# Eight single PSUM banks in one ring from the up-projection on, and the order of the final weights' rounding, in a hybrid encoder layer on one Trainium2 core

## The chip, the core and the metric

One NeuronCore of a Trainium2 chip runs the whole program. Its engines work at the same time, each through its own instructions in order: TensorE (PE, matrix multiplication; its weight loads are listed apart as PEld), VectorE (DVE), ScalarE (ACT), GpSimd (POOL) and SyncE (SP, which here only issues transfers). Matrix products land in PSUM, eight banks of 512 float32 values for each of the 128 partitions; DVE and ACT read them from there. Everything else lies in SBUF, and weights come from the device memory by DMA.

The metric is the time of one execution on the device in microseconds. A kernel is given by the median of its runs.

## The reference, cut to what matters

The model computes one layer for 512 prompt frames and 64 sample frames, in float32. After an adaLN modulation and a combined input projection come two recurrent mixers, an output projection and a residual. The change lies behind that, in the feed-forward part and the end:

```python
def conv_ffn(h, st, w_up, ffn_conv_w, ffn_conv_b, w_down):
    gate, val = jnp.split(h @ w_up, 2, axis=-1)
    gate_c, new_st = causal_dwconv(gate, st, ffn_conv_w)
    act = jax.nn.silu(gate_c + ffn_conv_b) * val
    return act @ w_down, new_st
...
        h = rmsnorm(x, norm2[l]) * (1 + sc2) + sh2
        f, s_f = conv_ffn(h, ffn_s[l], w_up[l], ffn_conv_w[l], ffn_conv_b[l], w_down[l])
        x = x + g2 * f
...
    y = rmsnorm(x, final_norm)
```

The width is 2048, the feed-forward width 5632, so `w_up` is 2048 x 11264 and `w_down` 5632 x 2048.

## The kernel before, in words

Channels lie on the partitions (16 tiles of 128 for the width, `KD`; 44 for the feed-forward width, `NFF`), frames along the free axis: two halves of 288 (`HT`), each with 256 prompt and 32 sample frames. float32 accuracy comes from splitting both operands into a rounded high part and a low part: ACT rounds (`wh`, line 1631), DVE subtracts (`wl`, line 1633), and PE adds three products, high-high, high-low and low-high (lines 1728 to 1730 in `up_product`, 648 and 650 in `mm6`).

Behind the mixers and the output projection (whose last eight-tile half, lines 2185 to 2192, ends at about 1266 us) the kernel has three stages:

- **Up-projection** (`up`, 44 units t = 0 to 43). Each unit computes one gate tile and one value tile by a Strassen-like scheme with seven products c = 0 to 6 over half of the depth, so each unit has seven sums of weights to prepare (`up_prep`, two steps ahead), seven products and seven outputs (`up_out`). A product is 8 x 3 matmuls. Its seven products go into three sums x, y and z, one PSUM bank each. The activation is written to device memory (`actd`); `pair_put` reads it back two tiles at a time, makes the combinations that the down-projection needs, and stores them (`cd`).
- **Down-projection** (units t = 44 to 75: four groups g of eight units u), the same scheme with 5 x 3 matmuls a product and 40 of the 44 depth tiles. The order of a unit's steps is 0, then step 6 of the unit before, then 2, 1, 3, 4, 5. `down_out` adds each sum to its place in SBUF on DVE (line 1924), in the first group it copies on ACT (line 1922). During units 1 to 4 of the first group `act_put` (lines 1963 to 1982) splits the last four activation tiles and stores them (`ald`). During the last group `down_end` closes the finished tiles on POOL (lines 1949, 1951, 1960) and ACT (line 1959).
- **Final** (`final`): for each half of the frames and each of the 16 output tiles m, PE adds the product of the last four depth tiles (12 matmuls of 320 or 256 columns), DVE adds it, scaled, to the residual (line 2042), and after every fourth m four transposes for each block of frames turn the result (line 2093), followed by the last RMS norm and the stores. `final_w` prepares the weights: for m below 6 by `wtile`, from 6 on into tiles `hw` of their own (ACT line 2065, DVE line 2067).

PSUM has two pools all this time. `pg` (line 110) has two double tiles of two banks each, handed out by `pgt` (line 663); `pm` (line 2139) has four single banks, handed out by `bank` (line 132). The up-projection takes its three sums from `pm`. In the down-projection even units and the last one take three banks of `pm`; odd units take two double tiles of `pg` and use the banks a0 (x), a1 (y) and b0 (z). The final products take a double tile for each two m, the transposes a bank of `pm`.

The order on each engine is made ahead of time by a planner which follows the program's order and its own estimate of times, lets a later instruction go first where an earlier one cannot start, and sets the semaphore waits. `issue_after(i)` holds an instruction behind instruction i on its engine; `high_priority` moves the block up. `self.round_of` and `self.split_of` are the latest weight rounding and subtraction of `up_split`, `self.load_of` the latest weight load.

Of the kernel before, what the change touches and what calls it, by code (L numbers as in the profile page):

```python
# [9 lines left out]
F32R = mybir.dt.float32r  # L10
I32 = mybir.dt.int32
AF = mybir.ActivationFunctionType
ALU = mybir.AluOpType
PSUM = bass.MemoryType.PSUM
# [9 lines left out]
NFF = 44  # L24
# [20 lines left out]
N_UNITS = NFF + KD // 2 * NCH  # L45
# [59 lines left out]
class Kern:  # L105
    def __init__(self, tc, ctx, i, o):
        self.tc, self.nc, self.ctx, self.i, self.o = tc, tc.nc, ctx, i, o
        self.n = 0
        self.cp = ctx.enter_context(tc.tile_pool(name="cp", bufs=1, side="left"))
        self.pg = ctx.enter_context(tc.tile_pool(name="pg", bufs=2, space=PSUM))  # L110
        self.c, self.scrap = {}, []
        self.now, self.chain, self.free = 0.0, None, dict.fromkeys(OP_US, 0.0)
        self.jv, self.ja = _Timed(self, _Sooner(tc, tc.nc.vector), "V"), _Timed(self, _Sooner(tc, tc.nc.scalar), "A")
        self.tv, self.ta = _Timed(self, tc.nc.vector, "V"), _Timed(self, tc.nc.scalar, "A")
        self.jt = _TimedPE(self, tc.nc.tensor)
        self.pool = _Timed(self, _InTurn(tc, tc.nc.gpsimd), "G")
# [1592 lines left out]
    def up_product(self, t, c):  # L1709

        w = HZ if t < NFF else HT
        if c == 0:
            if t < NFF or t % 2 == 0 or t == N_UNITS - 1:
                banks = [self.bank()[:, :w] for _ in range(3)]
            else:
                a, b = self.pgt(), self.pgt()
                banks = [a[:, 0, :w], a[:, 1, :w], b[:, 0, :w]]
            self.a[t, "banks"] = banks
            self.a.pop((t - 2, "banks"), None)
        T, (wh, wl) = self.nc.tensor, self.a.pop((t, "w", c))  # L1720
        ps = self.a[t, "banks"][(0, 2, 1, 0, 1, 2, 1)[c]][:, :HT if c in (T3, B22) else w]
        n = NPAIR if t < NFF else NJ
        for j in range(n):
            hi, lo, _ = self.combos[c, j] if t < NFF else self.dn[(t - NFF) // NPAIR, c, j]

            if c in (T3, B22):
                hi, lo = hi[:, :HT], lo[:, :HT]
            T.matmul(ps, wh[:, j], hi, start=(c < 3 and j == 0), stop=False, skip_group_check=True)  # L1728
            T.matmul(ps, wh[:, j], lo, start=False, stop=False, skip_group_check=True)  # L1729
            T.matmul(ps, wl[:, j], hi, start=False, stop=(j == n - 1), skip_group_check=True)  # L1730
# [232 lines left out]
    def act_put(self, n):  # L1963

        nc = self.nc
        r, f = [self.v_tile().rearrange("p h t -> p (h t)")[:, :2 * HT] for _ in range(2)]
        src, ald = self.actd[NFF - 4 + n], self.ald[n]
        with self.tc.issue_after(self.load_of):
            for h, b in ((0, 0), (1, HL)):
                nc.sync.dma_start(r[:, b:b + HP], src[:, h, :HP])  # L1970
            nc.sync.dma_start(r[:, HP:HL].rearrange("p (h t) -> p h t", h=2), src[:, :, HP:HT])
        yield
        hi = f.bitcast(F32R)
        with self.tc.issue_after(self.round_of):
            nc.scalar.activation(hi, r, AF.Copy)
        with self.tc.issue_after(self.split_of):
            nc.vector.tensor_tensor(r.bitcast(F32R), r, f, op=ALU.subtract)
        yield
        with self.tc.issue_after(self.load_of):
            nc.sync.dma_start(ald[:, 0], f)  # L1980
            nc.sync.dma_start(ald[:, 1], r)
        yield
# [23 lines left out]
    def final(self, acts, free):  # L2006

        wide = lambda n: [free.pop(0) for _ in range(n)]
        self.w_places, self.row_places = wide(20), wide(2)
        self.final_begin()
        w = []
        places = 2 * wide(12)
        late, behind, o = [], {}, self.o
        xs = [self.slot(p, F32, HT).rearrange("p h t -> p (h t)") for p in wide(2)]
        sampled = lambda m: xs[m // 8][:, m % 8 * 2 * HS:(m % 8 + 1) * 2 * HS]
        for h in range(2):
            cols = [(slice(0, HP), 0)]  # L2020
            toks = [(lambda m, h=h, b=b: self.x1[m][:, h, b:b + P], P, o["y_prompt"][0, h * HP + b:h * HP + b + P]) for b in range(0, HP, P)]
            if h == 0:
                cols.append((slice(HP, HL), 1))
                toks.append((sampled, 2 * HS, o["y_sample"][0]))
            span = (slice(0, HL), slice(HL, 2 * HT))[h]
            blocks = [(x, n, [places.pop(0) for _ in range(4)],
                       self.sp.tile([P, 8], F32, tag="fms", bufs=6, name=self.name("fms")), y) for x, n, y in toks]
            for m in range(KD):
                if m == len(w):
                    w += self.final_w(m, behind)  # L2030
                if m % 2 == 0:
                    ps = self.pgt()
                for k in range(4):
                    self.mm6(ps, w[m][0][:, k], w[m][1][:, k], [a[:, :, span] for a in acts[k]], k == 0, k == 3,
                             ((0, span.stop - span.start),), m % 2)
                for c, q in cols:
                    p = ps[:, m % 2, c]
                    if q == 0:
                        x = y = self.x1[m][:, h, c]
                    else:  # L2040
                        x, y, p = self.x1[m][:, :, HP:HT], self.halves(sampled(m)), self.halves(p)
                    self.nc.vector.scalar_tensor_tensor(y, p, self.mod[:, 5, m, q:q + 1], x,
                                                        op0=ALU.mult, op1=ALU.add)
                behind[m + KD * h] = self.nc.cur_bb.bb.instructions[-1]
                if late and m % 4 == LATE:
                    late.pop(0)()
                if m % 4 == 3:
                    late.append(lambda q=m // 4, blocks=blocks: self.final_part(q, blocks))
        while late:
            late.pop(0)()  # L2050

    def final_w(self, m, behind):

        src = self.w_down(NFF - 4, m)
        if m < 6:
            t = self.wtile(src)
            return [[x[:, :, j * P:(j + 1) * P] for x in t] for j in range(2)]
        raw = self.raw().rearrange("p (k n) -> p k n", k=4)
        w = [[pool.tile([P, 4, P], F32R, tag=tag, name=self.name("hw"))
              for pool, tag in self.w_places[2 * j:2 * j + 2]] for j in (m - 6, m - 5)]  # L2060
        with self.tc.high_priority(offset=AHEAD):
            self.nc.sync.dma_start(raw, src)
            for j, (hi, lo) in enumerate(w):
                r = raw[:, :, j * P:(j + 1) * P]
                self.nc.scalar.activation(hi, r, AF.Copy)
                with self.tc.issue_after(behind[m - 4]):
                    self.nc.vector.tensor_tensor(lo, r, hi.bitcast(F32), op=ALU.subtract)
        return w
# [44 lines left out]
def layer_kernel(tc, i, o):  # L2113
    nc = tc.nc
    with ExitStack() as ctx:
        K = Kern(tc, ctx, i, o)
        pool = lambda st, name, side="left", **kw: st.enter_context(tc.tile_pool(name=name, side=side, reuse_waits="tile", **kw))
# [15 lines left out]
        with ExitStack() as early:  # L2133
            K.wp = pool(early, "wp", "right", bufs=3)
            with ExitStack() as right:
                with ExitStack() as st:
                    K.pm = pool(st, "ph", bufs=2, space=PSUM, side=None)
                    K.head(pool(st, "head", bufs=1))
                K.pm = pool(ctx, "pm", bufs=4, space=PSUM, side=None)
                K.kp = pool(right, "kp", "right", bufs=1)  # L2140
                K.sp = pool(right, "sp", "right", bufs=2)
                K.load_consts(K.kp, [n for n in CONST_AT if n not in LONG + NARROW])
# [2 lines left out]
                with ExitStack() as st:  # L2145
# [10 lines left out]
                    w, ob = {}, []  # L2156
# [5 lines left out]
                    for m in range(KD):  # L2162
                        ps = K.pgt()
# [20 lines left out]
            for n, m in enumerate(order):  # L2184
                ps = K.pgt()
# [6 lines left out]
                if n % 2 == 1:  # L2192
                    (K.pair_early if n // 2 < N_EARLY else K.pair_begin)(n // 2)
            K.places += late
        K.ub = pool(ctx, "ub", "right", bufs=1)
        K.raws += [(K.ub, f"r{n}") for n in range(4, N_RAW)]
        K.xp = pool(ctx, "xp", bufs=1)
# [133 lines left out]
```

## Time and profile before

| what | value |
|---|---|
| median of 3 runs | 2802.99 us (2801.22 to 2802.99) |
| the profiled execution | 2801.18 us, its span 2799.5 us |
| PE busy | 2740.7 us, 98% of the span |
| DVE, ACT, POOL busy | 2279.0, 1311.2 and 461.6 us |
| granted PE clock, mean | 0.996 of full speed |
| up-projection, down-projection, final (from the order of time) | about 1266 to 2269, 2269 to 2722, 2722 to 2799.5 us |

A row of a group or of the order of time gives start and length in us, the engine, the line of the kernel, the operation, the tiles written and read (without buffer numbers), the shapes and the count; in brackets, the idle time of the engine before it and what ended it. A row of the waits gives who waited for whom: total us, times, longest. Tiles called `g` come from `pg`, tiles called `bank` from `pm`. Matmuls overlap: a row lasts about 0.3 us while the next one starts after 0.13, so a "busy" PE can still have lost time, and the distance from start to start is what counts.

### The profile page before, as it was taken

What the parts mean: (1) busy time and instruction counts of PE and PEld (TensorE: products, weight loads), DVE (VectorE), ACT (ScalarE), POOL (GpSimd) and SP (SyncE); (2) the same over time, 40 slices, a digit from 0 to 9 for tenths busy, and PEclk for the clock granted to TensorE, in tenths of its full rate; (3) what the DMA queues carried; (4) which work ended last, traced back from release to release, by engine and by line L of the source; (5) the groups of instructions that cost most, each with busy time, mean ns of one, the idle gap of its engine ahead of it and who ended that gap; (6) DMA issues with size and microseconds to landing.
All of it is one profiled execution on the core that took longest, in us unless ns stands there. A gap on an engine that the chain in (4) does not pass through costs nothing.

```text
span 2799.5 us, 52817 instructions
## 1 busy us (share of the span) xinstructions
PE 2740.7 (98%) x20596; PEld 2660.9 (95%) x20596; DVE 2279.0 (81%) x3697; ACT 1311.2 (47%) x2304; POOL 461.6 (16%) x436
## 2 busy tenths in 40 slices
PE   7999999999999999999999999999999999999998
PEld 4799999999999999999999999999999999999997
DVE  4578787777877887679899999999999976888885
ACT  4255555464544442355454545444444444333452
POOL 0001000010000000001333333333333300000240
PEclk9999999999999999999999999999999999999999
DMA  9965555554644657633555555554646495673751
GB/s 307 336 193 161 137 140 145 145 149 140 181 139 126 176 161 211 198 104 114 152 153 176 164 157 172 157 180 142 187 142 191 143 318 184 199 223 114 244 173 68
DMA packets 650270, 482.87 MB, mean 172 GB/s; under 512 B 66953, under 2 KB 575108, under 8 KB 650020
## 3 DMA queue, kind: packets, MB, share of 16 engines
q1 hardware_dynamic: 636916, 466.02, 55.6%
q10 hardware_dynamic: 13104, 13.47, 1.6%
q8 instruction: 162, 2.65, 0.4%
q14 instruction: 88, 0.72, 0.1%
HBM read 400.08 MB, written 79.32 MB: 171 GB/s over the span
## 4 chain that ended last, share of the span: by engine, by line
PE 81%; DVE 9%; DMA 3%; issue 3%; ACT 2%; POOL 1%; SPq 0%; ACTq 0%; DVEq 0%; POOLq 0%
PE g L648 17%; PE bank L1729 14%; PE bank L1728 14%; PE bank L1730 14%; PE g L650 8%; PE bank L2253 4%; DVE acc L2237 2%; PE g L1728 2%; PE g L1729 2%; PE g L1730 2%; PE bank L2249 1%; PE bank L870 1%; DVE wl L1633 1%; DVE wl L2237 1%; DVE m L2213 1%
## 5 line engine op out<-in xcount | busy, mean ns | idle before, releaser
L1729 PE MATMUL bank<-slot,wh 128*128 128x290 f32 (+1 forms) x3059 | 912.0, 298 | 0.0
L1728 PE MATMUL bank<-slot,wh 128*128 128x290 f32 (+1 forms) x3059 | 908.3, 297 | 2.0 <-ACT sqa L1600 1.2
L1730 PE MATMUL bank<-slot,wl 128*128 128x290 f32 (+1 forms) x3059 | 904.4, 296 | 0.2 <-DVE wl L1633 0.2
L1728 PEld LDWEIGHTS bank<-slot,wh 128*128 128x128 f32 x3059 | 576.3, 188 | 6.4 <-issue 3.6
L1730 PEld LDWEIGHTS bank<-slot,wl 128*128 128x128 f32 x3059 | 581.3, 190 | 0.9 <-DVE wl L1633 0.9
L1729 PEld LDWEIGHTS bank<-slot,wh 128*128 128x128 f32 x3059 | 578.3, 189 | 0.1
L648 PE MATMUL g<-hh,wh 128*128 128x288 f32 x2048 | 473.1, 311 | 1.9 <-ACT ts L2237 1.7
L1631 ACT ACTIVATE wh<-raw 128x1024 fp32r<-128x1024 f32 (+1 forms) x304 | 280.5, 923 | 363.4 <-PE bank L1729 268.0
L650 PE MATMUL g<-hh,wl 128*128 128x288 f32 x2048 | 442.0, 297 | 1.7 <-DVE wl L1028 1.7
L648 PE MATMUL g<-hl,wh 128*128 128x288 f32 x2048 | 442.5, 297 | 0.0
L1633 DVE TENSOR_TENSOR wl<-raw,wh 128x1024 fp32r<-128x1024 f32 (+1 forms) x304 | 370.0, 1218 | 71.0 <-ACT wh L1631 69.4
L648 PEld LDWEIGHTS g<-hh,wh 128*128 128x128 f32 x2048 | 325.3, 190 | 22.6 <-issue 14.5
L1631 ACT ACTIVATE wh<-s 128x1024 fp32r<-128x1024 f32 (+1 forms) x228 | 210.9, 927 | 285.3 <-DVE s L1644 103.4
L650 PEld LDWEIGHTS g<-hh,wl 128*128 128x128 f32 x2048 | 330.8, 189 | 5.1 <-issue 3.1
L648 PEld LDWEIGHTS g<-hl,wh 128*128 128x128 f32 x2048 | 330.6, 189 | 3.2 <-issue 2.3
L1633 DVE TENSOR_TENSOR wl<-s,wh 128x1024 fp32r<-128x1024 f32 (+1 forms) x228 | 251.6, 1105 | 14.7 <-ACT wh L1631 13.5
L2237 ACT ACTIVATE wh<-raw 128x1024 fp32r<-128x1024 f32 x135 | 142.8, 1058 | 201.5 <-PE g L648 197.4
L2237 DVE SCALAR_TENSOR_TENSOR acc<-aw,ct,acc 128x512 f32<-128x512 f32 x284 | 201.1, 742 | 3.9 <-DMA aw<-in_w_ada_dram 3.9
L2237 DVE TENSOR_TENSOR wl<-raw,wh 128x1024 fp32r<-128x1024 f32 x135 | 164.3, 1217 | 47.8 <-ACT wh L2237 45.0
L1852 POOL TENSOR_TENSOR j<-j,j 128x288 f32<-128x288 f32 (+1 forms) x120 | 185.6, 1553 | 84.4 <-ACT j L1856 82.1
L1728 PE MATMUL g<-slot,wh 128*128 128x288 f32 x525 | 156.6, 298 | 1.7 <-DVE slot L1924 1.7
L1729 PE MATMUL g<-slot,wh 128*128 128x288 f32 x525 | 155.1, 296 | 0.0
(341 smaller groups left out, 4014.9 us busy)
## 6 DMA issues: line engine op xcount, KB each, us to landing
raw<-in_w_up_dram SPq DMA_DIRECT2D x176, 512.0 KB
raw<-in_w_in_dram SPq DMA_DIRECT2D x100, 512.0 KB
raw<-in_w_down_dram SPq DMA_DIRECT2D x128, 320.0 KB
aw<-in_w_ada_dram SPq DMA_DIRECT2D x79, 512.0 KB
slot<-cd SPq DMA_DIRECT2D x140, 288.0 KB
cd<-j SPq DMA_DIRECT2D x120, 288.0 KB
xr<-in_w_ada_dram SPq DMA_DIRECT2D x49, 512.0 KB
hraw<-in_w_ada_dram SPq DMA_DIRECT2D x40, 512.0 KB
```

Source lines behind the costliest of these rows:

```text
L648: T.matmul(ps[:, h if bank is None else bank, :n], wh, x[:, h, :n], start=f, stop=False)
L650: T.matmul(ps[:, h if bank is None else bank, :n], wl, ah[:, h, :n], start=False, stop=stop)
L870: T.matmul(ps[32 * k:32 * k + 32, :w], cs[:, k0 + k], got[n][k // per][:, k % per], start=(k0 == 0), stop=(k0 == KD - 4))
L1631: self.nc.scalar.activation(hi, src, AF.Copy)
L1633: self.nc.vector.tensor_tensor(lo, src, hi.bitcast(F32), op=ALU.subtract)
L1728: T.matmul(ps, wh[:, j], hi, start=(c < 3 and j == 0), stop=False, skip_group_check=True)
L1729: T.matmul(ps, wh[:, j], lo, start=False, stop=False, skip_group_check=True)
L1730: T.matmul(ps, wl[:, j], hi, start=False, stop=(j == n - 1), skip_group_check=True)
L1852: minus = lambda out, a, b: G.tensor_tensor(out, a, b, op=ALU.subtract)
L2213: return f(*a, **kw)
L2237: return f(*a, **kw)
L2253: return self.engine.matmul(out, *a, **kw)
```

## The change

It has three parts.

1. Both PSUM pools go into a stack of their own, `K.psum`. After the output projection this stack is closed, and a new pool `pu` of eight single banks takes their place for all that follows; `bank` hands them out. In the down-projection every unit takes three single banks, odd ones too. In the final stage each m has a bank of its own, and the transposes take theirs from the same eight.
2. In `act_put`, the subtraction of line 1977 (128 x 576, four times in all) moves from DVE, where it was held behind the latest weight subtraction, to POOL, without a hold.
3. In `final_w`, the rounding of the `hw` weights on ACT (line 2065) is held behind `self.round_of`, at that point the last weight rounding of the last down unit.
Loads, shapes, the number of matmuls and the arithmetic are the same.

```diff
-        self.pg = ctx.enter_context(tc.tile_pool(name="pg", bufs=2, space=PSUM))
+        self.psum = ctx.enter_context(ExitStack())
+        self.pg = self.psum.enter_context(tc.tile_pool(name="pg", bufs=2, space=PSUM))
...
         if c == 0:
-            if t < NFF or t % 2 == 0 or t == N_UNITS - 1:
-                banks = [self.bank()[:, :w] for _ in range(3)]
-            else:
-                a, b = self.pgt(), self.pgt()
-                banks = [a[:, 0, :w], a[:, 1, :w], b[:, 0, :w]]
-            self.a[t, "banks"] = banks
+            self.a[t, "banks"] = [self.bank()[:, :w] for _ in range(3)]
...
         with self.tc.issue_after(self.round_of):
             nc.scalar.activation(hi, r, AF.Copy)
-        with self.tc.issue_after(self.split_of):
-            nc.vector.tensor_tensor(r.bitcast(F32R), r, f, op=ALU.subtract)
+        nc.gpsimd.tensor_tensor(r.bitcast(F32R), r, f, op=ALU.subtract)
...
-                if m % 2 == 0:
-                    ps = self.pgt()
+                ps = self.bank().unsqueeze(1)
                 for k in range(4):
                     self.mm6(ps, w[m][0][:, k], w[m][1][:, k], [a[:, :, span] for a in acts[k]], k == 0, k == 3,
-                             ((0, span.stop - span.start),), m % 2)
+                             ((0, span.stop - span.start),))
                 for c, q in cols:
-                    p = ps[:, m % 2, c]
+                    p = ps[:, 0, c]
...
-                self.nc.scalar.activation(hi, r, AF.Copy)
+                with self.tc.issue_after(self.round_of):
+                    self.nc.scalar.activation(hi, r, AF.Copy)
...
-                K.pm = pool(ctx, "pm", bufs=4, space=PSUM, side=None)
+                K.pm = pool(K.psum, "pm", bufs=4, space=PSUM, side=None)
...
             K.places += late
+        K.psum.close()
+        K.pm = pool(ctx, "pu", bufs=8, space=PSUM, side=None)
         K.ub = pool(ctx, "ub", "right", bufs=1)
```

## The prediction, made before the result was known

> **What bounds the kernel now.** I read the page's head first, then the sums by stretch, then the waits of the matmul engine (PE), then the order of time at each of those waits.
>
> ```profile
> span 2799.5 us, 52817 instructions
> ...
> 1290.00:2240.00 950.00, 949.80 (x7034) 945.80 (x7033) 865.95 (x966) 466.76 (x584) 326.52 (x286) 1.00 0.54 161
> ...
> 2605.00:2710.00 105.00, 103.34 (x769) 102.12 (x768) 96.88 (x132) 47.98 (x76) 41.07 (x25) 1.00 0.63 186
> ```
>
> In a row of sums the columns are length, busy time and count of PE, weight loads, DVE, ACT and POOL, then the granted clock and the DMA's share. PE is the bound, at a granted clock of 1.00: from 1290 to 2240 us its 7034 matmuls follow each other every 0.135 us, busy 949.8 of 950 us. The change touches nothing ahead of the up-projection (1266 us), so all it can win is the idle time of PE behind that. This is what the waits of PE show there:
>
> ```profile
> PE g L648 <- DVE slot L2042: 2.8, 2, 2.6
> ...
> PE g L1728 <- DVE slot L1924: 1.7, 3, 0.6
> ...
> PE bank L1728 <- ACT hw L2065: 0.5, 1, 0.5
> ```
>
> A matmul's row is about 0.3 us long while the next starts 0.13 us later, so these rows show a stall some 0.15 us too small; below I count from start to start.
>
> **The change part by part.** Double tiles become single banks: first in the down-projection. Unit t with odd t holds its three sums in two double tiles of `pg`: x and y share one. The second product of such a unit writes y while the vector engine (DVE) still has to read x:
>
> ```profile
> 2651.89 0.29 PE L1730 MATMUL bank<-slot,wl 128*128 128x288 f32 x1
> 2652.15 0.45 DVE L1924 TENSOR_TENSOR slot<-g,slot 128x288 f32<-128x288 f32 x1
> 2652.74 0.37 PE L1728 MATMUL g<-slot,wh 128*128 128x288 f32 x1 [0.55 <-DVE slot L1924]
> ...
> 2404.94 0.40 PE L1728 MATMUL g<-slot,wh 128*128 128x288 f32 x1
> 2405.17 0.30 PE L1729 MATMUL g<-slot,wh 128*128 128x288 f32 x1
> ```
>
> The sum that DVE reads at 2652.15 was finished a whole product (2 us) earlier, and it lies in the other bank of the tile that PE wants; PE starts 0.14 us after that read ends (2652.60). Start to start is 0.85 us instead of 0.13, a loss of 0.72. The waits count three of these, in the last odd units, so 3 x 0.71 = 2.1 us. In the other 12 odd units the wait is only grazed: at 2404.94 two starts lie 0.23 instead of 0.13 apart, 0.10 us each, 1.2 us together. Even units have single banks already, and the waits name no `bank` tile for line 1924. With single banks the reader of x holds back nobody but the next product on x, three products later. From below: DVE's lateness itself stays, and if it takes the waits over, nothing of the 2.1 is won; from above 3.3 us. I take 3.3.
>
> The final stage: its 16 output blocks m are computed two to a double tile.
>
> ```profile
> 2722.57 0.54 PE L648 MATMUL g<-slot,wh 128*128 128x320 f32 x2
> ...
> 2725.29 0.45 PE L648 MATMUL g<-slot,wh 128*128 128x320 f32 x2
> 2725.39 1.04 ACT L2237 ACTIVATE wh<-raw 128x1024 fp32r<-128x1024 f32 x1
> 2726.46 1.23 DVE L2237 TENSOR_TENSOR wl<-raw,wh 128x1024 fp32r<-128x1024 f32 x1 [1.65 <-ACT wh L2237]
> 2727.60 0.67 DVE L2042 SCALAR_TENSOR_TENSOR slot<-g,mod,slot 128x256 f32<-128x256 f32 x2
> 2728.33 0.56 PE L648 MATMUL g<-slot,wh 128*128 128x320 f32 x2 [2.58 <-DVE slot L2042]
> ```
>
> PE stands from 2725.4 to 2728.33, until the residual of m=0 (line 2042) is read out of the same double tile. That read is late because DVE, which works in order, waits for a rounding on ScalarE (ACT) that belongs to m=4. Two starts (2725.29 and one 0.15 later) and then 2728.33: 3.04 us for two steps of 0.15, a loss of 2.75. Single banks take it away: m=1 then needs no reader. Next in line is m=4, whose weights are complete at 2727.69 (2726.46 + 1.23); PE began m=0 at 2722.57, and four blocks of 12 steps of 0.15 (20 starts lie between 2722.57 and 2725.44) bring it to 2729.8, or 2729.1 with the 0.70 of the next paragraph: later than 2727.69, so nothing waits. Bounds 1.5 (if m=4 or m=6 then waits for DVE for as long as one of its 1.23 us splits) and 2.75; I take 2.75.
>
> ```profile
> 2768.62 0.28 PE L650 MATMUL g<-slot,hw 128*128 128x256 f32 x1
> 2769.22 0.51 PE L648 MATMUL g<-slot,wh 128*128 128x256 f32 x2 [0.31 <-DVE fms L2237]
> ...
> 2770.74 1.04 PE L2093 MATMUL bank<-consts,slot 128*128 128x128 f32 x8
> 2772.01 0.50 PE L648 MATMUL g<-slot,hw 128*128 128x256 f32 x2 [0.23 <-DVE slot L2042]
> ```
>
> Twice more a block waits for DVE, busy with the first half's outputs: 0.60 - 0.12 = 0.48, and 2772.01 against an eighth transpose that began about 2771.51 and needs 0.11, so 0.39. With eight banks both go: 0.87 us (bounds 0 and 0.87).
>
> The held rounding (the `hw` weights, line 2065):
>
> ```profile
> 2717.20 1.15 ACT L2065 ACTIVATE hw<-raw 128x512 fp32r<-128x512 f32 x2 [2.72 <-DMA raw<-in_w_down_dram]
> 2718.25 0.72 ACT L1631 ACTIVATE wh<-raw 128x640 fp32r<-128x640 f32 x1
> 2719.01 0.82 DVE L1633 TENSOR_TENSOR wl<-raw,wh 128x640 fp32r<-128x640 f32 x1 [2.69 <-ACT wh L1631]
> 2719.51 0.29 PE L1730 MATMUL bank<-slot,wl 128*128 128x288 f32 x1
> 2719.75 0.45 DVE L1924 TENSOR_TENSOR slot<-bank,slot 128x288 f32<-128x288 f32 x1
> 2720.34 0.37 PE L1728 MATMUL bank<-slot,wh 128*128 128x288 f32 x1 [0.54 <-ACT hw L2065]
> ```
>
> ACT stands 2.72 us for the final weights' transfer with the last unit's own rounding (line 1631) queued behind it. DVE waits 2.69 us for that rounding with the read of the last unit's y (2719.75) queued behind it, and PE's last product waits for y: 0.83 - 0.13 = 0.70 us. Held behind line 1631, the two roundings still come when their data is there (2717.20), and line 1631 can use the 2.72 us. Gain 0.70, bounds 0 and 0.70. The splits of `hw` on DVE keep their own hold.
>
> The subtraction that moves to GpSimd (POOL), four times, and what of the SyncE (SP) queue hangs on it:
>
> ```profile
> L1977 DVE TENSOR_TENSOR v<-v,v 128x576 fp32r<-128x576 f32 x4 | 3.0, 759 | 0.2
> L1960 POOL TENSOR_TENSOR slot<-slot,v 128x576 f32<-128x576 f32 x16 | 26.6, 1666 | 22.5 <-issue 19.3 <-ACT slot L1959 2.9 <-POOL slot L1951 0.2
> L1633 DVE TENSOR_TENSOR wl<-raw,wh 128x640 fp32r<-128x640 f32 x20 | 16.5, 823 | 14.0 <-ACT wh L1631 13.7 <-DMA raw<-in_w_down_dram 0.3
> L1686 DVE TENSOR_TENSOR s<-s,raw 128x640 f32<-128x640 f32 x5 | 4.1, 821 | 0.1
> L1686 DVE TENSOR_TENSOR s<-s,raw 128x640 f32<-128x640 f32 x7 | 11.6, 1650 | 0.1
> 2290.00:2360.00 70.00, 70.00 (x525) 69.42 (x524) 49.96 (x69) 35.56 (x64) 0.00 (x0) 1.00 0.64 190
> ```
>
> DVE gives up 4 x 0.76 us, POOL, idle in this stretch, takes 4 x 1.67. The store behind it is issued 0.9 us later, and SP's next loads with it; they are of the next units. Against that, DVE's own work stretches while POOL reads: the same line 1686 takes 0.82 us here and 1.65 in 2605 to 2710, where POOL is busy. In this stretch DVE idles 20 of 70 us, 14.0 of them just ahead of its splits, so I count 0; without that cover it is 4 x 0.83 = 3.3 us. [...]
>
> The new pool at 1266 us:
>
> ```profile
> 1266.02 0.29 PE L1728 MATMUL bank<-slot,wh 128*128 128x290 f32 x1
> 1266.37 0.93 DVE L2237 SCALAR_TENSOR_TENSOR slot<-g,mod,slot 128x512 f32<-128x512 f32 x2
> ...
> 1272.10:1291.50 19.40, 17.96 (x128) 17.27 (x128) 19.23 (x38) 9.47 (x20) 0.10 (x1) 1.00 0.35 99
> ...
> 1276.11 0.40 PE L1728 MATMUL bank<-slot,wh 128*128 128x290 f32 x1 [1.17 <-ACT sqa L1600]
> ...
> 1289.53 0.40 PE L1728 MATMUL bank<-slot,wh 128*128 128x290 f32 x1 [0.28 <-DVE v L1751]
> ```
>
> The first unit now starts in banks that the last output-projection tile may still hold; its residual is read until 1267.30. The calls of `pgt` before it are even in number (18 + 36 + 50 + 32), so by a plain ring that tile is the second one, and unit 0's x takes a bank of the first: cost 0, at worst 1.3 us. The 1.2 us wait at 1276.11 (a fourth bank that the norm still holds) goes. But DVE is busy 19.23 of the 19.40 us from 1272.1 to 1291.5 and PE meets it again at 1289.53; what PE gains at 1276 it waits there. I take 0 for the head, bounds -1.3 and +1.3.
>
> **The sum.** 3.3 + 2.75 + 0.87 + 0.70 = 7.6 us. The profiled execution took 2801.2 us (the span and 1.7 around it), 1.8 under the runs' median of 2803.0. So 2793.6 for a run like the profiled one, and 2795.4 against the median, which I predict.
>
> **The rivals.** *DVE takes the waits over.* It is busy 96.88 of 105 us in the closing units, and with the false waits gone PE asks for its splits sooner. Then the 2.1 us of the three odd units and the 0.87 come back as waits for splits, and 7.6 - 3.0 = 4.6 is left: 2798.4. For it: that share; against it: even units of the same stage show no hole.
>
> *The stretched DVE work comes onto the path: slower.* POOL is busy in the closing units, and DVE's instructions of one shape take longer there than in 2290 to 2360 (0.82 us each):
>
> ```profile
> L1633 DVE TENSOR_TENSOR wl<-raw,wh 128x640 fp32r<-128x640 f32 x29 | 27.1, 933 | 1.7 <-ACT wh L1631 1.6
> L1633 DVE TENSOR_TENSOR wl<-s,wh 128x640 fp32r<-128x640 f32 x22 | 22.2, 1015 | 0.5 <-ACT wh L1631 0.5
> ```
>
> That is 29 x 0.11 + 22 x 0.19 on these splits and 7 x 0.83 on line 1686, 13.2 us in all, now hidden because the planner fills PE's waits with pieces of a neighbouring product. If PE in strict order met all of them, the result would be 2795.4 + 13.2 = 2808.6; it turns slower from the point where more than 7.6 of the 13.2 us, over half, are exposed. Against it: DVE still has 8.1 idle us in the stage, and even units run in strict order today.
>
> [...]
>
> *The change does not do what it says:* the order of the down units was never ruled by the shared tile, but by DVE's lateness alone. Then only 0.70 and some of the 2.75 is won, about 2800.
>
> **How the numbers follow.** The forecast has 0.66, the first rival 0.18, the slower one 0.07, the moved subtraction 0.04, the last 0.05; a little of the forecast's share (0.02) falls short of faster by its own bounds, and a little of the first rival's (0.03), with a low price of 1.5 us, reaches it. Without the slower case and with the head's and the rest's bounds (7.6 + 1.3, and some 20 more starts in the final stage that lie 0.1 us late like the one at 2404.94, 2 us) the range is 2791.0 to 2801.0. A measurement can tell 0.2%, 5.6 us, from no change: 2797.4 divides faster from the same. Faster 0.66 - 0.02 + 0.03 = 0.67, same 0.26, slower 0.07.
>
> **What would show it.** Right: no wait of PE on line 1924 or 2042 in the waits, no `g` tile behind 1266 us, even and odd units of equal length, line 1631 ahead of 2065 at the last unit, PE's last transposes some 7.6 us earlier, and the 11 us behind them as they are. Wrong: waits of PE for `wl` from line 1633 in the closing units, a hole ahead of m=4 or m=6 in the final stage, PE idle at 1266 us.

## The result and the profile after

The median of four runs is 2790.52 us (2789.53 to 2792.04), that of the kernel before on the same chip 2802.99 us (2801.22 to 2805.27). The ratio is 0.9956 with a 95% interval of 0.9944 to 0.9968, which is 9.0 to 15.7 us. Forecast were 7.6 us (2795.4) and a range down to 2791.0, so the kernel is faster than the range allowed by 0.5 us. The profiled execution took 2792.04 us, 9.1 us less than the profiled one of before.

The head of the page and the sums by stretch of the changed kernel:

```profile
span 2790.3 us, 52838 instructions
...
1290.00:2240.00 950.00, 949.90 (x7033) 945.81 (x7033) 865.52 (x965) 466.30 (x583) 325.79 (x286) 1.00 0.54 161
2290.00:2360.00 70.00, 70.00 (x529) 70.00 (x529) 47.63 (x66) 35.63 (x64) 5.73 (x4) 1.00 0.64 190
2605.00:2710.00 105.00, 105.00 (x787) 104.61 (x786) 101.01 (x135) 49.19 (x78) 41.30 (x26) 1.00 0.64 191
2719.00:2779.00 60.00, 59.71 (x466) 59.43 (x464) 42.46 (x94) 22.61 (x55) 7.72 (x7) 1.00 0.24 76
```

From 2605 to 2710 us PE now issues 787 matmuls instead of 769, and it is busy all of the 105 us (103.34 before). The waits of PE, behind 1266 us all of over 0.15 us that are left:

```profile
PE bank L1726 <- DVE wl L1634: 1.0, 2, 0.7
...
PE bank L1724 <- DVE v L1747: 0.6, 1, 0.6
...
PE bank L651 <- DVE wl L2234: 0.3, 1, 0.3
```

(Lines have moved: 1724 to 1726 are the products of `up_product`, 1634 the split, 1920 the sum of `down_out`, 649 and 651 `mm6`, 2036 the residual, 2060 the final rounding.) No wait on line 1920 and none on the residual is left. The order of time in the last odd units and at the start of the final stage:

```profile
2650.45 0.30 PE L1726 MATMUL bank<-slot,wl 128*128 128x288 f32 x1
2650.59 0.29 PE L1724 MATMUL bank<-slot,wh 128*128 128x288 f32 x1
...
2651.55 0.44 DVE L1920 TENSOR_TENSOR slot<-bank,slot 128x288 f32<-128x288 f32 x1
...
2716.80 0.63 ACT L2060 ACTIVATE hw<-raw 128x512 fp32r<-128x512 f32 x1 [2.41 <-DMA raw<-in_w_down_dram]
2717.34 1.04 ACT L2234 ACTIVATE wh<-raw 128x1024 fp32r<-128x1024 f32 x1
2718.41 1.23 DVE L2234 TENSOR_TENSOR wl<-raw,wh 128x1024 fp32r<-128x1024 f32 x1 [3.04 <-DMA fn<-in_final_norm_dram]
2718.87 0.54 PE L649 MATMUL bank<-slot,wh 128*128 128x320 f32 x2
2719.69 0.42 PE L651 MATMUL bank<-slot,wl 128*128 128x320 f32 x1 [0.29 <-DVE wl L2234]
...
2724.87 1.83 DVE L2036 SCALAR_TENSOR_TENSOR slot<-bank,mod,slot 128x256 f32<-128x256 f32 x6
```

DVE is no earlier than before, rather later. These are the products whose rows of before stand in the prediction (2652.15 and 2652.74): the one that PE now begins at 2650.59 is the same in order, 2850 matmuls into the down-projection. DVE starts to read the finished sum at 2651.55, 0.96 us after that; before, it was 0.13 us after the moment at which PE would have begun it. But PE does not wait for the read any more. In the final stage DVE reads m=0 only at 2724.87, when PE is three blocks further on (12 steps of 0.148 us a block, from 2718.87), and PE goes on at its pace. One new wait stands there: the low part of m=0's own weights is not split yet when PE wants it (2719.69). The rounding of these weights (2717.34) stands on ACT behind a `hw` rounding that waited 2.41 us for its transfer; whether it could have run ahead of that one was not tried.

For sizes I split each trace at four points that can be read in its order of time: the start of the first matmul of the up-projection, that of its last, the first final matmul, the last end on PE. The column on the right goes on to the end of the span, some 11 us further.

| kernel | ratio to before (95%) | first up product at | up | down | final | first up product to the end |
|---|---|---|---|---|---|---|
| before | 1 | 1266.0 | 1002.3 | 454.3 | 66.0 | 1533.5 |
| changed | 0.9956 (0.9944–0.9968) | 1267.0 | 1001.8 | 450.0 | 60.4 | 1523.3 |
| changed, once more | 0.9952 (0.9941–0.9964) | 1266.1 | 1001.8 | 449.2 | 60.2 | 1522.3 |
| no hold | 0.9966 (0.9954–0.9978) | 1269.7 | 1001.7 | 451.7 | 59.8 | 1524.3 |
| subtraction on DVE | 0.9952 (0.9940–0.9964) | 1261.3 | 1001.9 | 450.2 | 60.2 | 1523.3 |
| old pools, hold, subtraction on POOL | 1.0001 (0.9993–1.0010) | 1270.0 | 1002.2 | 454.4 | 66.0 | 1533.4 |
| single banks in the final stage only | 0.9978 (0.9970–0.9987) | 1265.6 | 1002.6 | 456.1 | 59.8 | 1529.6 |
| single banks in up and down only | 0.9987 (0.9978–0.9997) | 1268.3 | 1001.6 | 453.5 | 64.4 | 1530.4 |
| odd units: x and y in tiles of their own | 0.9988 (0.9979–0.9997) | 1265.9 | 1002.2 | 451.5 | 66.1 | 1530.7 |
| odd units: x and z share | 1.0015 (1.0006–1.0024) | 1266.7 | 1002.2 | 456.7 | 67.6 | 1537.4 |
| final blocks in double tiles of their own | 0.9995 (0.9987–1.0004) | 1265.7 | 1002.4 | 454.5 | 65.0 | 1533.0 |
| old rings, nothing shared, hold | 0.9968 (0.9956–0.9979) | 1264.0 | 1002.4 | 449.4 | 63.5 | 1526.5 |
| ring of five | 0.9954 (0.9941–0.9966) | 1262.3 | 1001.8 | 449.6 | 60.3 | 1522.8 |
| changed, activation a step later | 0.9943 (0.9930–0.9955) | 1266.2 | 997.9 | 449.3 | 60.1 | 1518.3 |

The stretch ahead of the first up product, which no edit touches, lies between 1261.3 and 1270.0 us in these traces. So a single span says little about 2 us, while the column on the right repeats within 1 us for the changed kernel. By it the change is worth 10.1 and 11.2 us; the 12.5 us of the medians agree with that within their interval. Of the eleven executions of the kernel in which x and z share, one took 5014.8 us, at a granted clock of 0.86; it is in no ratio.

### The profile page after: what moved, and what is told of

It is laid out like the page before. It is cut to its first block, busy times and chain, and to the rows that moved or that the text cites. A ratio compares the mean times of both kernels' runs of the same rounds, so it can differ in the third digit from the quotient of the medians.

```text
span 2790.3 us, 52838 instructions
## 1 busy us (share of the span) xinstructions
PE 2738.5 (98%) x20596; PEld 2662.4 (95%) x20596; DVE 2278.2 (82%) x3693; ACT 1309.7 (47%) x2304; POOL 466.4 (17%) x440
## 4 chain that ended last, share of the span: by engine, by line
PE 80%; DVE 10%; DMA 3%; issue 3%; ACT 2%; POOL 1%; SPq 0%; ACTq 0%; DVEq 0%; POOLq 0%
PE g L649 16%; PE bank L1725 16%; PE bank L1724 16%; PE bank L1726 15%; PE g L651 8%; PE bank L2250 4%; DVE acc L2234 2%; DVE wl L1634 2%; PE bank L2246 1%; PE bank L649 1%; PE bank L871 1%; DVE wl L2234 1%; DVE m L2210 1%; DVE slot L1920 1%; PE bank L651 1%
## 5 line engine op out<-in xcount | busy, mean ns | idle before, releaser
L1725 PE MATMUL bank<-slot,wh 128*128 128x290 f32 (+1 forms) x3584 | 1068.2, 298 | 0.0
L1724 PE MATMUL bank<-slot,wh 128*128 128x290 f32 (+1 forms) x3584 | 1063.9, 297 | 0.7 <-DVE v L1747 0.6
L1726 PE MATMUL bank<-slot,wl 128*128 128x290 f32 (+1 forms) x3584 | 1060.7, 296 | 1.2 <-DVE wl L1634 1.0
L1726 PEld LDWEIGHTS bank<-slot,wl 128*128 128x128 f32 x3584 | 680.5, 190 | 2.8 <-DVE wl L1634 2.4
L1724 PEld LDWEIGHTS bank<-slot,wh 128*128 128x128 f32 x3584 | 675.5, 188 | 5.0 <-issue 4.5
L1725 PEld LDWEIGHTS bank<-slot,wh 128*128 128x128 f32 x3584 | 677.5, 189 | 0.1
L2234 DVE SCALAR_TENSOR_TENSOR acc<-xr,ct,acc 128x512 f32<-128x512 f32 x196 | 141.7, 752 | 0.0
L1920 DVE TENSOR_TENSOR slot<-bank,slot 128x288 f32<-128x288 f32 x184 | 83.2, 452 | 33.5 <-PE bank L1726 32.0
```

The lines of the kernel that those rows point to most:

```text
L1920: V.tensor_tensor(dst, ps, dst, op=ALU.add)
L2234: return f(*a, **kw)
```

## The experiments

**The change once more,** without any edit.

> The changed kernel once more, in more rounds. Its profiled execution ended 9.1 us ahead of the profiled one of before (2792.0 against 2801.2), its median 12.5 us ahead. If the trace is right the paired ratio comes out near 0.9965 (10 us: 0.5 us in the up-projection, 4.3 in the down-projection, 5.9 in the final stage, with 1.0 us lost by chance ahead of 1266 us); if the medians are right, near 0.9955, and some 2 to 3 us are in none of my terms.

2790.11 us (2785.73 to 2792.48), ratio 0.9952: the result repeats. The interval of the ratio, 10.1 to 16.5 us, has room for the 11.2 us of its trace as well as for the 12.5 us of the first medians. So it is not shown that 2 or 3 us lie outside the terms.

**Without the hold.** The final roundings are no longer issued behind the last unit's:

```diff
-                with self.tc.issue_after(self.round_of):
-                    self.nc.scalar.activation(hi, r, AF.Copy)
+                self.nc.scalar.activation(hi, r, AF.Copy)
```

> The change without the hold of the final weights' rounding. Theory (my term of 0.70 us): 0.7 us slower than the whole change, with a hole ahead of the last unit's last product of about 0.8 us in the trace. Rival (the hold is worth more because it also orders what follows on ScalarE): 2 us or more. Rival (with single banks the late rounding hurts nobody): 0.

2794.97 us, ratio 0.9966. The intervals overlap, so the size is read from the trace, at the last unit:

```profile
2717.78 1.15 ACT L2059 ACTIVATE hw<-raw 128x512 fp32r<-128x512 f32 x2 [3.53 <-DMA raw<-in_w_down_dram]
2719.59 0.82 DVE L1634 TENSOR_TENSOR wl<-raw,wh 128x640 fp32r<-128x640 f32 x1 [2.75 <-ACT wh L1632]
2720.34 0.45 DVE L1920 TENSOR_TENSOR slot<-bank,slot 128x288 f32<-128x288 f32 x1
2720.93 0.37 PE L1724 MATMUL bank<-slot,wh 128*128 128x288 f32 x1 [1.36 <-ACT hw L2059]
```

It is the chain of the kernel before, only longer: ACT stands 3.53 us for the transfer instead of 2.72, and PE loses 1.52 us (start to start, less 0.135) instead of 0.70. With single banks PE reaches this place 3.9 us earlier than before, counted from the first up product, the rounding that waits for the transfer only 3.1 us earlier. So the hold is worth more beside the single banks than without them: 1.52 us, less the 0.45 that the changed kernel loses at m=0. From the first up product on this kernel takes 1.0 and 2.0 us longer than the two executions of the changed one: more than the 0.7 us expected, and the rival's 2 us or more are not excluded.

**The subtraction back on DVE**, in the changed kernel:

```diff
-        nc.gpsimd.tensor_tensor(r.bitcast(F32R), r, f, op=ALU.subtract)
+        with self.tc.issue_after(self.split_of):
+            nc.vector.tensor_tensor(r.bitcast(F32R), r, f, op=ALU.subtract)
```

> The change with the four subtractions of act_put back on VectorE behind the latest split. Theory (VectorE idles 20 of 70 us there): the same time within 0.5 us. [...] Rival (the move is part of the gain): slower by 1 us or more.

Ratio 0.9952, and 1523.3 us from the first up product on: no difference. The groups of the changed kernel in 2290 to 2360:

```profile
L1634 DVE TENSOR_TENSOR wl<-raw,wh 128x640 fp32r<-128x640 f32 x21 | 18.1, 864 | 16.9 <-ACT wh L1632 15.7 <-DMA raw<-in_w_down_dram 1.2
...
L1972 POOL TENSOR_TENSOR v<-v,v 128x576 fp32r<-128x576 f32 x4 | 5.7, 1432 | 59.2 <-ACT v L1971 46.7 <-DMA slot<-cd 12.4
```

A subtraction takes 1.43 us on POOL (the prediction took 1.67 from another line). DVE's splits of this shape take 864 ns on the mean instead of the 823 of before, 0.9 us over 21 of them: four, each of which begins about 0.36 us before the end of one of the subtractions on POOL, take 1.03 to 1.05 us, the others 0.81 to 0.83. DVE idles 16.9 us ahead of the splits, and that covers it.

**Old pools with the other two edits:** the hold and the subtraction on POOL go into the kernel before, the pools stay as they were.

```diff
-        with self.tc.issue_after(self.split_of):
-            nc.vector.tensor_tensor(r.bitcast(F32R), r, f, op=ALU.subtract)
+        nc.gpsimd.tensor_tensor(r.bitcast(F32R), r, f, op=ALU.subtract)
...
-                self.nc.scalar.activation(hi, r, AF.Copy)
+                with self.tc.issue_after(self.round_of):
+                    self.nc.scalar.activation(hi, r, AF.Copy)
```

> The old pools with the two other edits alone (hold of the rounding, subtraction on GpSimd). Theory: 0.7 us faster than before, 2802.3 on a median of 2803.0, the three holes on line 1924 and the hole of 2.75 us in the final stage still there. Rival (the pools do not carry the gain): 3 us or more of the 12 are here.

Ratio 1.0001. At the last unit the hold does what it should: DVE waits for PE there, and no longer PE for DVE:

```profile
2721.21 0.83 DVE L1633 TENSOR_TENSOR wl<-raw,wh 128x640 fp32r<-128x640 f32 x1 [0.18 <-ACT wh L1631]
2722.56 0.46 DVE L1924 TENSOR_TENSOR slot<-bank,slot 128x288 f32<-128x288 f32 x1 [0.52 <-PE bank L1730]
```

The 0.77 us of that place (0.70 and 0.07 at the start behind it) are gone, but this execution lost about 0.9 us more than the one of before in the first down units (2272 to 2287), where a weight transfer is late by a varying amount: the first waits there cost between 0 and 0.9 us in these traces, whatever the kernel. 0.7 us are 0.00025 of the time and lie inside the interval, so the timing neither shows nor denies them. The three waits on line 1924 (1.7 us together) and the long one of the final stage (2.4 us) are still there, as expected, so these two edits do not carry the gain.

**Single banks in the final stage only.** Up and down keep the old pools; between the stages these are closed and eight single banks opened.

```diff
         K.up()
+        K.psum.close()
+        K.pm = pool(ctx, "pu", bufs=8, space=PSUM, side=None)
         K.down()
...
-                if m % 2 == 0:
-                    ps = self.pgt()
+                ps = self.bank().unsqueeze(1)
```

> Old double tiles through the down-projection; eight single banks from the start of the final stage on, without the two other edits. Theory (final stage 5.9 us in the trace: 2.75 + 0.87 as in my sum, and some 2 us of small late starts that I had left out): 5.9 us faster than before, 2797. Rival (my sum was right for this stage, the rest is elsewhere): 3.6 us, 2799.4.

Ratio 0.9978. The final stage itself falls by 6.2 us. Opening the pool at this place has a price of its own, ahead of the first final block:

```profile
2723.66 0.45 DVE L1925 TENSOR_TENSOR slot<-bank,slot 128x288 f32<-128x288 f32 x1
...
2724.21 0.53 PE L649 MATMUL bank<-slot,wh 128*128 128x320 f32 x2 [1.73 <-ACT hw L2065]
```

(Lines are one further here: 1925 is the sum of `down_out`.) The profile names a rounding as the last releaser. But PE starts 0.10 us behind the end of DVE's read of the last unit's sum (2724.11), which fits the new pool giving m=0 the bank of that sum; that was not tried by itself. It costs 1.9 us and hides part of the gain: 3.9 us from the first up product on, 5.8 with the 1.9 added.

**Single banks in up and down only**, and the old kind of pools opened again for the final stage; no hold.

```diff
         K.up()
+        K.psum.close()
+        K.pg = ctx.enter_context(tc.tile_pool(name="pg2", bufs=2, space=PSUM, reuse_waits="tile"))
+        K.pm = pool(ctx, "pm2", bufs=4, space=PSUM, side=None)
         K.down()
```

> Eight single banks for the up- and the down-projection; the final stage goes back to two double tiles and four single banks, without the two other edits. Theory: 0.5 us in the up-projection and 3.6 in the down-projection, 4.1 us faster than before, 2798.9; the hole of 2.75 us at the second final block stays. Rival (the stages share one gain, DVE takes it over in the final stage): under 2 us.

Ratio 0.9987. The down stage loses the same 1.9 us at its end as the last kernel, and 1.67 us at the last product, where the hold is missing. What is left between them is small: from 2300 to the last unit 1.4 us of lost starts instead of 4.9. The expected wait of 2.75 us at the second final block has shrunk to 1.1, probably because PE, held up for 1.9 us just before, comes to it later; that was not tried by itself.

**Is it the sharing or the number of banks?** In the kernel before, with its old pools, the odd units take the same two double tiles, but x and y one each, and z a single bank:

```diff
-                banks = [a[:, 0, :w], a[:, 1, :w], b[:, 0, :w]]
+                banks = [a[:, 0, :w], b[:, 0, :w], self.bank()[:, :w]]
```

> Old pools, old final stage; only the three sums of an odd down unit get a tile each: one bank of each double tile, and a single bank. Theory (what costs is that two sums share a tile, not the number of free banks): 3.3 us faster than before, no hole on line 1924. Rival (it is the eight banks in one ring that let PE go on): no difference from before. Rival (VectorE's lateness): no difference, the holes stay as waits for the splits.

Ratio 0.9988. Of its waits of PE:

```profile
PE g L648 <- DVE slot L2042: 2.9, 2, 2.6
...
PE bank L1728 <- ACT hw L2065: 1.5, 1, 1.5
```

The waits on line 1924 are gone without one bank more. Between 2300 and the last unit PE loses 0.85 us instead of 4.9, less than the 1.1 of the changed kernel. So the cause is the shared tile. Of the 4 us, 0.94 come back at once at the last product (1.64 instead of 0.70): again the rounding that waits for the transfer comes less early (2.8 us, from the first up product on) than PE (3.8 us).

**The opposite:** x and z share a double tile.

```diff
-                banks = [a[:, 0, :w], a[:, 1, :w], b[:, 0, :w]]
+                banks = [a[:, 0, :w], b[:, 0, :w], a[:, 1, :w]]
```

> Old pools; the odd down units put x and z into one double tile, and y alone into the other. Theory (a shared tile): product 3 (into x) comes directly behind product 1 (into z) and now has to wait for the read of z, 0.3 us of the matmul's end, 0.45 us of the read and 0.15 us of signalling, 0.9 us less what the planner fills: slower than the old kernel by 2 to 10 us over 15 units. Rival (sharing is harmless): the same as before.

Ratio 1.0015, slower. Of its waits of PE:

```profile
PE g L1730 <- DVE wl L1633: 3.2, 4, 0.9
...
PE bank L1728 <- ACT hw L2065: 1.3, 1, 1.3
...
PE g L1728 <- DVE slot L1924: 0.5, 1, 0.5
```

The wait moves to another place, and with it splits come late that did not before. Which pairs share decides the price: the down stage takes 2.4 us more than before, at the low end of the 2 to 10 us expected. (1.6 us of the longer final stage have a cause of their own, below.)

**Sharing or depth in the final stage.** Each final block takes a double tile of its own and uses one half, in the kernel before:

```diff
-                if m % 2 == 0:
-                    ps = self.pgt()
+                ps = self.pgt()
...
-                             ((0, span.stop - span.start),), m % 2)
+                             ((0, span.stop - span.start),), 0)
```

> The kernel before, with one edit: in the final stage each output block m takes a double tile of its own and uses only its first half, so that no two blocks share a tile; still two tiles in the ring. Theory (sharing of a tile costs the small late starts and the two waits of 0.4 to 0.5 us, but the first long wait needs depth as well): with a ring two deep m=2 needs the residual of m=0, which is read until 2728.2 us, while PE would be there 24 steps of 0.148 us after 2722.6, at 2726.1; so 2.2 of the 2.75 us stay, 0.5 go, and the 0.87 and about 2 us of late starts go: the final stage falls from 66.0 to about 62.7 us, the time by 3.3 us, ratio 0.9988. Rival 1 (sharing is all): final stage 60.4 us, ratio 0.998. Rival 2 (only the number of banks counts): final stage 65.5 to 66.1 us, ratio 1.000.

Ratio 0.9995, final stage 65.0 us where 62.7 were expected. m=1 no longer waits, but m=2 does, and then PE runs slowly for a while. PE's rows in order of time, then the sums by stretch of the same place:

```profile
2725.99 0.31 PE L650 MATMUL g<-slot,wl 128*128 128x320 f32 x1
2729.07 0.53 PE L648 MATMUL g<-slot,wh 128*128 128x320 f32 x2 [2.77 <-DVE slot L2041]
```

```profile
2726.00:2729.00 3.00, 0.30 (x3) 0.03 (x1) 1.89 (x4) 3.00 (x7) 1.63 (x2) 1.00 0.64 203
2729.00:2730.20 1.20, 1.13 (x7) 1.16 (x8) 0.51 (x2) 0.94 (x3) 1.20 (x2) 0.91 0.03 9
2730.20:2733.20 3.00, 3.00 (x13) 3.00 (x12) 1.24 (x4) 0.94 (x2) 0.58 (x1) 0.50 0.00 0
```

A ring two deep does not cover DVE's lateness: the long wait stays, now 2.93 us. The granted clock then falls to 0.50; 13 starts lie 0.267 us apart instead of 0.148, which costs 1.55 us. Without it the final stage would be 63.5 us.

**Old rings, nothing shared, and the hold:** the edits of the last kernel, of x and y in tiles of their own, and the hold together, in the kernel before.

> The kernel before with its two old rings kept (four singles, two doubles): odd down units take x, y and z from three different tiles, each final block a double tile of its own with one half used, and the final roundings are held as in the changed kernel; the subtraction stays on DVE and no pool is opened. Theory (sharing and the hold are all in the down stage, depth matters only for the first final blocks): from the first up product on, 3.75 us of down losses and the 0.7 us at the last product go, and some 3 us in the final stage: about 7.5 us less than before, ratio 0.9973; what it lacks against the changed kernel (about 3 us) is the wait of m=2. Rival (eight banks in one ring are needed): less than 4 us won, ratio 0.9986 or more.

Ratio 0.9968; 7.0 us less from the first up product on, of 7.5 expected. Down is as short as in the changed kernel (449.4 us). What it lacks is this wait of PE, and 0.39 us at one later block:

```profile
PE g L648 <- DVE slot L2041: 2.7, 2, 2.5
```

So sharing explains the down stage and the late starts of the final stage; the one long wait of the final stage needs depth as well.

**How deep?** The changed kernel with `bufs=5` for its ring instead of `bufs=8`.

> The changed kernel with five single banks in its ring instead of eight. Theory (what counts is that no two sums share a tile; in the final stage m needs the reader of the block or transpose five places earlier, some 17 us back): the same as the changed kernel within 1 us from the first up product on, ratio to before 0.995 to 0.996. Rival (the depth of eight is what the change lives on): 3 us or more come back, ratio 0.9966 or more.

Ratio 0.9954, 1522.8 us from the first up product on, the same as with eight. Five are enough: when DVE reads m=0, PE is in block m=3. Three and four were not tried.

**The next hole.** The changed kernel still loses starts in every second up unit. The order of time at one of them:

```profile
1373.17 0.94 DVE L1781 SCALAR_TENSOR_TENSOR v<-v,ca 128x512 f32<-128x512 f32 x2
...
1374.03 0.45 DVE L1742 TENSOR_TENSOR g<-bank,p 128x290 f32<-128x290 f32 x1
...
1374.36 0.30 PE L1726 MATMUL bank<-slot,wl 128*128 128x290 f32 x1
...
1374.63 0.37 PE L1724 MATMUL bank<-slot,wh 128*128 128x288 f32 x1
1374.83 0.30 PE L1725 MATMUL bank<-slot,wh 128*128 128x288 f32 x1
```

DVE's read of a sum stands behind the activation of the unit before (line 1781), and the next product goes into the same sum: a true dependence, which no ring removes. The edit issues the activation one step later:

```diff
-            if 0 < t < NFF and c == 2 or t == NFF and c == 1:
+            if 0 < t < NFF and c == 3 or t == NFF and c == 1:
```

> The changed kernel with one more edit: the gate and activation of the unit before (up_act), which stand on the vector engine ahead of the read of sum y, are issued one step later, at c=3 instead of c=2, for the up units. In the changed kernel's trace every second up unit loses 0.13 us and then 0.07 us at the product that waits for that read (20 times, 4.0 us in all). Theory (that read is late because of the work queued ahead of it): these go, the up stage falls from 1001.8 to about 997.8 us, ratio to before about 0.9942. Rival 1: the later place delays the next read by as much, no difference, 0.9956. Rival 2: the activation then arrives late for the unit's store or for the last up unit, slower than the changed kernel by 1 us or more.

2786.25 us (2785.58 to 2786.74), ratio 0.9943; the up stage falls to 997.9 us, as expected, and the same stretch now holds 7062 matmuls instead of 7033:

```profile
1290.00:2240.00 950.00, 949.99 (x7062) 949.53 (x7061) 852.65 (x969) 468.25 (x585) 319.37 (x286) 1.00 0.54 162
```

It is the fastest kernel of this study, by the traces 4 to 5 us ahead of the changed one from the first up product on; side by side the two were not timed.

## Why the prediction fell short

The mechanism was the one forecast; the sum was too small. Each term as the prediction put it, against lost time counted from start to start (distance less the ordinary one of that shape) in the two traces:

| term | predicted | in the traces |
|---|---|---|
| shared tiles in the down units | 3.3 | 3.75 (4.89 lost before, 1.14 after, 2300 us to the last unit) |
| long wait at m=1 | 2.75 | 2.74 |
| two waits in the second half | 0.87 | 0.87 |
| hold of the final roundings | 0.70 | 0.77 at the last product, less 0.45 new at m=0 |
| small late starts of the final stage | 0, 2 in the range | 2.2 (32 losses, 2.9 us, before; 8, 0.7 us, after) |
| head, 1266 to 1305 us | 0 | 0.66 (2.97 lost before, 2.31 after) |
| moved subtraction | 0 | 0 |

These rows together give 10.5 us; the traces, from the first up product on, 10.1, with 0.2 us more than before behind the last matmul.

- **The failed step is "some 20 more starts in the final stage that lie 0.1 us late".** The prediction saw them, and put them into the range and not into the sum, with no row that spoke against counting them. They are worth 2.2 us, and with them the sum would have been 9.8. They are the same shared tile, only grazed, which in the down units the sum did count (12 x 0.10). The kernel with old rings and nothing shared shows it: in its final stage only some eight are left, as in the changed kernel, and it has no ring of eight.
- **The down term** was a little small. In each of the 12 odd units that are only grazed it counted one late start of 0.10 us; the trace has two, 0.14 us together, and 0.21 in the four of the first group, where the read is ACT's copy. It also left out the 0.07 us behind each of the three holes. The cause was right: the kernel with x and y in tiles of their own, on the old pools, lost the waits on line 1924.
- **The hold** had its sign and its chain right, and its size for the kernel before. Beside the single banks it guards against 1.52 us, since PE gains 3.9 us up to there and the rounding that waits for the transfer 3.1. The prediction priced each part against the trace of before only. Nor did it see what is late next: it looked ahead of m=4 and m=6; the wait came at m=0's own low weights (0.45 us), whose rounding stands behind a held one.
- **The head** came out between its bounds. The wait at 1276.11 went, and part of it came back at the next one:

```profile
1289.83 0.37 PE L1724 MATMUL bank<-slot,wh 128*128 128x290 f32 x1 [0.63 <-DVE v L1747]
```

- **The median.** The sum was made against the profiled execution and carried over to the median, which lay 1.8 us above it. The changed kernel's profiled execution lies 1.5 above its median. The 8.7 us by which the untouched first stage varies are more than either, so of the gap between 7.6 and 12.5 us some 2.5 to 3.6 belong to the terms above and the rest cannot be told from that spread. The range had a slip of its own: 7.6 + 1.3 + 2 us below the median before is 2792.1, not 2791.0, so by its own bounds the miss is 1.6 us.
- **The rivals.** DVE taking the waits over: PE has no wait of over 0.15 us, the least that the waits list, from 2605 to 2710, though DVE's busy time rose from 96.88 to 101.01 of 105 us. Exposed stretching of DVE's work is not seen. The moved subtraction felt, with its chance of 0.04: no run shows a price of it on the path; beside it four splits grew by about 0.2 us each, under DVE's idle time. That the change does not do what it says is refuted by the two kernels that only changed which sums share.

## What to carry to other kernels

A tile of two banks is one thing to the program's order: whoever writes one half waits for the reader of the other, even where the two have nothing to do with each other. Look for waits of PE on a reader whose sum was finished a product earlier, give each sum a tile of its own, and only then ask for depth, which here had to reach past the time that the reader is late, and no further (five banks did what eight did). When one part makes the engine earlier, price a hold or a prefetch against the new time: here the engine gained 3.9 us up to the last product, the transfer behind which a rounding stood only 3.1, and the wait grew from 0.70 to 1.52 us. And each late start seen in a row of before belongs into the sum.

## What the runs showed of the hardware

In two of these kernels a stall of PE of about 3 us cost more than its length. In the kernel with final blocks in double tiles of their own (3.08 us from start to start) and in the one where x and z share (2.935 us) the granted clock went to 0.50 soon after PE had started again, within 1.0 and 0.4 us, for some 3 us; each lost about 1.6 us by it. The second of them, in the sums by stretch:

```profile
2732.00:2734.70 2.70, 2.70 (x12) 2.70 (x11) 0.00 (x0) 1.34 (x3) 1.23 (x1) 0.50 0.00 1
```

In the kernel before (2.89 us), with x and y in tiles of their own (2.934 us) and with old rings and nothing shared (2.77 us) the clock stayed at 1.00. So two stalls of equal length can fall on the two sides. Nor is 2.9 us an edge for every place. Ahead of the up-projection, in the changed kernel, PE stood for 2.15 us from start to start (until 648.50), and the clock was 0.50 from 649.2 to 652.6, behind eight small matmuls within some 1 us; after 2.02 us (until 68.67), in the same trace, it stayed at 1.00. So the length of one stall does not settle it, and what does is not shown.

The wait of 2.89 us which the change removed was of a length that paid this price in one kernel and not in another. Whether other executions of the kernel before paid it is open: only one of them has a trace.
